# Chain of chunks: two engines' reads of one accumulator bank declared independent of each other

## The chip, the cores and the metric

The kernel runs on one core of a Trainium2 chip. The metric is the time of one execution in microseconds (us), as the device measures it. Before the change it is 1743.63 us (median of three runs, 1741.31 to 1744.07).

The engines are named as in the profile: PE is TensorE (its matmuls; PEld is its loading of weights), DVE is VectorE, ACT is ScalarE, POOL is GpSimd, SP is SyncE, which here only issues transfers. PE writes its products into accumulator banks; DVE and ACT read them out.

## The reference, cut to what matters

One layer of an encoder is computed for 1024 prompt frames and 64 sample frames: modulated norm, one input projection, two groups of heads (a delta-rule recurrence, "RWKV", and a forgetting attention, "FoX"), output projection, and a gated feed-forward network. The change lies in the recurrence, which for each of 8 heads is

```python
def step(s, inp):
    r_t, w_t, k_t, v_t, kk_t, a_t = inp
    sa = jnp.einsum('bhvk,bhk->bhv', s, -kk_t)
    s = (s * w_t[:, :, None, :]
         + sa[..., None] * (kk_t * a_t)[:, :, None, :]
         + v_t[..., None] * k_t[:, :, None, :])
    return s, jnp.einsum('bhvk,bhk->bhv', s, r_t)
...
ys_state = lax.scan(step, s0, xs)
...
x = x + gt1[:, None] * (jnp.concatenate([y_rwkv, y_fox], axis=-1) @ w_out)
ffn = (jax.nn.silu(h2 @ w_ffn_gate) * (h2 @ w_ffn_up)) @ w_ffn_down
```

`s` is a 64x64 state per head. The kernel computes the scan in chunks of 64 frames.

## The kernel before

**Halves and stages.** The frames are worked in two halves: half 0 has 512 (8 chunks), half 1 has 512 and the 64 sample frames (9 chunks, in matmuls of 288 columns). For each half the projections (L294 to L296, three products per tile because each factor is split in a high and a low part), the four pairs of RWKV heads, and the preparation of the attention are traced piece by piece, in an order that a string of letters gives. Then come attention, output projection (with attention of half 1), feed-forward and its last product (`pd`, L1264).

**The chain of chunks.** `rwkv_b` handles one pair of heads, `j`, of one half: the first head lies in partitions 0 to 63, the second in 64 to 127. After some preparation it walks over the chunks, and each chunk needs the state that the chunk before it left. There are 8 such chains (4 pairs, 2 halves), with 68 chunks in all. One chunk is, in the names of the program:

- `pR` (PE, L597), from the state and values `sv`; it is read out to `R`, the first head by DVE (L599), the second by ACT (L600);
- `pY` (PE, L608), a first part of the output, which nobody waits for at once;
- `pSA` (PE, L610), from `R`; it is read out into `sv`, the first head by DVE (L611), the second by ACT (L612);
- `pS` (PE, L613), from `sv`; DVE adds it twice (L617, one instruction a head) to the decayed state `sd`, which POOL has made (L604), and so writes the state for the next chunk;
- `pY` again (L618). After every fourth chunk `pY` is read out to `y`, one head by ACT and one by DVE (L623).

So each of `pR`, `pSA` and `pY` is one accumulator bank of which DVE reads one half of the partitions and ACT the other. 68 pairs of reads are at `pR`, 68 at `pSA`, 20 at `pY`.

**What sets the order.** The programming framework records the instructions, finds which must wait for which, and orders each engine's instructions with a list scheduler that works by its own estimate of when inputs are ready. Between the products of a chain it therefore puts other work on PE, above all projections (`pmm`) and, in the last chain, attention of half 0 (`psc`, `ppt`, `pav`). An engine then takes its instructions strictly in that order. Its rule for accumulator banks is that instructions of different engines on one bank are put in order, whatever partitions they touch: of the two reads of a pair, the second engine waits for the first.

Of the kernel before, what the change touches and what calls it, by code (L numbers as in the profile page):

```python
# [11 lines left out]
ALU = mybir.AluOpType  # L12
# [52 lines left out]
class K:  # L65
# [351 lines left out]
    def rwkv_a(self, hf, j, z, d):  # L417
# [79 lines left out]
                nc.sync.dma_start(d[0:ng].rearrange("g x s t -> (g x) s t")[:, o, o], t[r])  # L497
        return zv, rk, kb, pc, bon, At, dw, du

    def rwkv_b(self, hf, j, st):  # L500

        zv, rk, kb, pc, bon, At, dw, du = st
        nc, vc, O = self.nc, self.vc, self.O
# [57 lines left out]
        sv = self.rpool.tile([P, 9, 2, 64], F32, tag="sv", name="sv")  # L561
        S = self.state[j]
        for c in range(0, nch, 4):
            m = min(4, nch - c)
# [4 lines left out]
        for t0 in range(0, nch, 8):  # L569

            m = min(8, nch - t0)
# [9 lines left out]
        hsl = [slice(0, 64), slice(64, 128)]  # L581

        def put_state(c, src):
            nc.vector.tensor_copy(sv[hsl[0], c, 0], src[hsl[0]])
            nc.scalar.copy(sv[hsl[1], c, 1], src[hsl[1]])
        y = self.slot(name="y", tag="sb")
        put_state(0, S)
        py = None
        for c in range(nch):
            if c == 8:  # L590
                nc.sync.dma_start(O["state_p"][j], S)
                st = self.rpool.tile([P, 64], F32, tag="st", name="st")
                nc.sync.dma_start(st, self.A["state"][j])
                put_state(8, st)

            pr = self.ps([P, 2, 64], tag="ch", name="pR")
            nc.tensor.matmul(pr, At[:, c, 0], sv[:, c], start=True, stop=True)  # L597
            R = self.rpool.tile([P, 64], F32, tag="R", name="R")
            nc.vector.tensor_copy(R[hsl[0]], pr[hsl[0], 0])  # L599
            nc.scalar.copy(R[hsl[1]], pr[hsl[1], 1])  # L600

            sd = self.rpool.tile([P, 64], F32, tag="sd", name="sd")
            for h in range(2):
                nc.gpsimd.tensor_scalar(sd[hsl[h]], sv[hsl[h], c, h], pc[hsl[h], c], None, op0=ALU.mult)  # L604
            pS = self.ps([P, 2, 64], tag="ch", name="pS")
            if c % 4 == 0:
                py = self.ps([P, 4, 2, 64], tag="rb", name="pY")
            nc.tensor.matmul(py[:, c % 4], sv[:, c], rk[:, c], start=True, stop=False, skip_group_check=True)  # L608
            pa = self.ps([P, 64], tag="ch", name="pSA")
            nc.tensor.matmul(pa, inv[:, c], R, start=True, stop=True)  # L610
            nc.vector.tensor_scalar(sv[hsl[0], c, 0], pa[hsl[0]], -1.0, None, op0=ALU.mult)  # L611
            nc.scalar.mul(sv[hsl[1], c, 1], pa[hsl[1]], -1.0)  # L612
            nc.tensor.matmul(pS, kbt[:, c], sv[:, c], start=True, stop=True)  # L613
            last = c == 7 or c == nch - 1
            s0, s1 = (S[hsl[0]], S[hsl[1]]) if last else (sv[hsl[0], c + 1, 0], sv[hsl[1], c + 1, 1])
            for h, d in enumerate((s0, s1)):
                nc.vector.scalar_tensor_tensor(d, pS[hsl[h], h], pc[hsl[h], c], sd[hsl[h]], op0=ALU.mult, op1=ALU.add)  # L617
            nc.tensor.matmul(py[:, c % 4], sv[:, c], At[:, c, 1], start=False, stop=True, skip_group_check=True)  # L618
            if c % 4 == 3 or c == nch - 1:
                m = c % 4 + 1  # L620
                cb = c - m + 1
                for h, cp in enumerate((nc.scalar.copy, nc.vector.tensor_copy)):
                    cp(y[hsl[h], cb * 64:(c + 1) * 64].rearrange("p (c t) -> p c t", t=64), py[hsl[h], 0:m, h])  # L623
        if hf.smp:
            nc.sync.dma_start(O["state_s"][j], S)
        return y, bon
# [1075 lines left out]
```

## Time and profile before

| | |
|---|---|
| time, median of 3 runs | 1743.63 us (1741.31 to 1744.07) |
| the profiled execution's own time | 1735.94 us |
| its span, first to last instruction | 1734.2 us |
| PE, PEld busy | 1663.8 us (96%), 1447.9 us (83%) |
| DVE, ACT, POOL busy | 1126.6 us (65%), 729.1 us (42%), 180.8 us (10%) |
| mean granted PE clock | 0.981 |
| the 8 chains run from | 149 us to 728 us |

The profile is of one execution. In its listings a row of the timeline has start, duration, engine, line, operation, output<-inputs and shape, and in square brackets how long the engine had been idle and who ended that. In a list of waits a row reads: who waited, for whom, total us, how often, the longest. A waiting engine costs time only where work behind it is late for somebody. PE's busy time counts a matmul from its start to the end of its pipeline, so that consecutive matmuls overlap, and small gaps between starts are hidden in it.

### The profile page before, as it was taken

How to read it: one execution, taken by the hardware profiler on the slowest of the kernel's cores; microseconds unless marked ns; L12 is line 12 of the kernel's file. 1: busy time of each engine (PE TensorE's matmuls, PEld its weight loads, DVE VectorE, ACT ScalarE, POOL GpSimd, SP SyncE). 2: the span in 40 equal slices, each digit the busy share in tenths (PEclk: the TensorE clock that was granted, in tenths of full speed). 3: DMA queues.
4: the chain of work that ended last, by engine and by line, in shares of the span. 5: the costliest groups of instructions: out<-in, count | busy, mean ns of one | idle time of the engine just before them, and what ended most of it. 6: DMA issues, size and time to landing. Idle time of an engine off the chain costs nothing.

```text
span 1734.2 us, 33257 instructions
## 1 busy us (share of the span) xinstructions
PE 1663.8 (96%) x12893; PEld 1447.9 (83%) x12893; DVE 1126.6 (65%) x2574; ACT 729.1 (42%) x1532; POOL 180.8 (10%) x412
## 2 busy tenths in 40 slices
PE   5999999999999999889999989999999999999999
PEld 3676766688888888766888889999999999999998
DVE  6676676757686753876877686666666655555545
ACT  4534454553454445765776453333233223211210
POOL 2102121131221212300210000000000000000000
PEclk9999999999899999989999999999999999999999
DMA  8535457632233344566553333222222224433213
GB/s 314 149 95 137 142 140 207 175 93 56 55 76 75 95 121 136 157 194 177 151 177 136 127 115 101 75 75 75 76 75 82 78 87 143 161 98 98 95 37 122
DMA packets 133581, 207.09 MB, mean 119 GB/s; under 512 B 62126, under 2 KB 70350, under 8 KB 133422
## 3 DMA queue, kind: packets, MB, share of 16 engines
q1 hardware_dynamic: 133422, 204.95, 39.3%
q8 instruction: 102, 1.67, 0.4%
q14 instruction: 57, 0.47, 0.1%
HBM read 157.65 MB, written 47.25 MB: 118 GB/s over the span
## 4 chain that ended last, share of the span: by engine, by line
PE 82%; DVE 7%; ACT 7%; DMA 2%; issue 2%; SPq 1%; POOL 0%; DVEq 0%; ACTq 0%; POOLq 0%
PE pd L1264 15%; PE pfc L1153 8%; PE pfe L1153 8%; PE pfa L1153 7%; PE pmm L294 5%; PE pmm L296 5%; PE pmm L295 5%; PE pfb L1153 4%; PE pav L962 2%; PE pbs L375 2%; PE pA L464 2%; PE ppt L940 2%; PE po L294 1%; PE po L295 1%; PE po L296 1%
## 5 line engine op out<-in xcount | busy, mean ns | idle before, releaser
L294 PE MATMUL pmm<-hhi,whi 128*128 128x288 f32 (+1 forms) x624 | 220.7, 354 | 0.7 <-ACT pb L317 0.7
L295 PE MATMUL pmm<-hlo,whi 128*128 128x288 f32 (+1 forms) x624 | 218.2, 350 | 0.0
L296 PE MATMUL pmm<-hhi,wlo 128*128 128x288 f32 (+1 forms) x624 | 218.0, 349 | 0.0
L212 ACT CAST whi<-wraw 128x1024 fp32r<-128x1024 f32 (+2 forms) x116 | 99.3, 856 | 214.4 <-PE pd L1264 167.0
L1264 PE MATMUL pd<-ah,wlo 128*128 128x512 f32 (+1 forms) x528 | 173.5, 329 | 0.0
L1264 PE MATMUL pd<-al,whi 128*128 128x512 f32 (+1 forms) x528 | 173.2, 328 | 0.0
L1264 PE MATMUL pd<-ah,whi 128*128 128x512 f32 (+1 forms) x528 | 173.0, 328 | 0.0
L1268 DVE SCALAR_TENSOR_TENSOR x1t<-pd,mod,x1t 128x512 f32<-128x512 f32 x192 | 91.4, 498 | 110.6 <-PE pd L1264 110.0
L294 PEld LDWEIGHTS pmm<-hhi,whi 128*128 128x128 f32 x624 | 120.3, 193 | 13.5 <-ACT pb L317 2.0
L296 PEld LDWEIGHTS pmm<-hhi,wlo 128*128 128x128 f32 x624 | 120.3, 193 | 10.9 <-issue 1.7
L295 PEld LDWEIGHTS pmm<-hlo,whi 128*128 128x128 f32 x624 | 120.4, 193 | 9.6 <-issue 0.7
L216 DVE TENSOR_TENSOR wlo<-wraw,whi 128x1024 fp32r<-128x1024 f32 (+2 forms) x108 | 103.8, 961 | 26.0 <-ACT whi L212 25.6
L1153 PE MATMUL pfc<-hh,hS 128*128 128x256 f32 (+1 forms) x352 | 102.0, 290 | 4.4 <-ACT hh L1055 4.4
L1264 PEld LDWEIGHTS pd<-al,whi 128*128 128x128 f32 x528 | 99.4, 188 | 7.7
L1264 PEld LDWEIGHTS pd<-ah,whi 128*128 128x128 f32 x528 | 99.3, 188 | 7.7
L1264 PEld LDWEIGHTS pd<-ah,wlo 128*128 128x128 f32 x528 | 99.2, 188 | 7.4
L1153 PE MATMUL pfc<-hl,hS 128*128 128x256 f32 (+1 forms) x352 | 102.3, 290 | 0.0
L1153 PE MATMUL pfc<-hh,lS 128*128 128x256 f32 (+1 forms) x352 | 102.0, 290 | 0.0
L1153 PE MATMUL pfa<-hl,whi 128*128 128x256 f32 (+1 forms) x352 | 101.8, 289 | 0.0
L1153 PE MATMUL pfa<-hh,whi 128*128 128x256 f32 (+1 forms) x352 | 101.7, 289 | 0.0
L1153 PE MATMUL pfa<-hh,wlo 128*128 128x256 f32 (+1 forms) x352 | 101.4, 289 | 0.0
L604 POOL TENSOR_SCALAR sd<-sv,pc 64x64 f32<-64x64 f32 x136 | 72.0, 529 | 172.9 <-DVE sv L617 156.6
(360 smaller groups left out, 4402.0 us busy)
## 6 DMA issues: line engine op xcount, KB each, us to landing
wraw<-in_w_in_dram SPq DMA_DIRECT2D x52, 512.0 KB
wada<-in_w_ada_dram SPq DMA_DIRECT2D x48, 512.0 KB
as<-actscr SPq DMA_DIRECT2D x22, 544.0 KB
wraw<-in_w_gate_dram SPq DMA_DIRECT2D x22, 512.0 KB
wraw<-in_w_up_dram SPq DMA_DIRECT2D x22, 512.0 KB
wraw<-in_w_down_dram SPq DMA_DIRECT2D x40, 256.0 KB
wraw<-in_w_out_dram SPq DMA_DIRECT2D x16, 512.0 KB
actscr<-sg SPq DMA_DIRECT2D x22, 288.0 KB
```

The costliest lines, as they stand in the source:

```text
L212: nc.scalar.copy(hi, src)
L216: eng.tensor_tensor(lo, src, hi.bitcast(F32), op=ALU.subtract)
L294: nc.tensor.matmul(ps[0:M, 0:n], whi[:, k, 0:M], xhi[:, k, off:off + n], start=(k == 0), stop=False)
L295: nc.tensor.matmul(ps[0:M, 0:n], whi[:, k, 0:M], xlo[:, k, off:off + n], start=False, stop=False)
L296: nc.tensor.matmul(ps[0:M, 0:n], wlo[:, k, 0:M], xhi[:, k, off:off + n], start=False, stop=(k == kt - 1))
L375: nc.tensor.matmul(ps[:, 0:n], w, x[:, off:off + n], start=True, stop=True)
L464: nc.tensor.matmul(pa[h][:, i], kb[hp, c + i], rk[hp, c + i], start=True, stop=True)
L604: nc.gpsimd.tensor_scalar(sd[hsl[h]], sv[hsl[h], c, h], pc[hsl[h], c], None, op0=ALU.mult)
L940: nc.tensor.transpose(pt[0:rows, b - b0, t * P:t * P + qn], p[0:qn, pc:pc + rows], self.ident[0:qn, 0:qn])
L1153: nc.tensor.matmul(ps, l[:, k], r[:, s, k], start=(first and k == 0 and y == 0), stop=(k == 3 and y == 2), skip_group_check=True)
L1264: nc.tensor.matmul(ps[:, 0:n], w[:, i], x[:, t:t + n], start=(i == 0 and y == 0), stop=(i == len(fs) - 1 and y == 2))
L1268: nc.vector.scalar_tensor_tensor(dst, ps[:, so - off:so - off + l], self.mod[:, 40 + o, b:b + 1], dst, op0=ALU.mult, op1=ALU.add)
```

## The change

A helper declares to the framework that, of two instructions, neither has to wait for the other. It is applied to the three pairs of reads in the loop over the chunks. The instructions themselves, their shapes and their engines stay. Since the helper is new, lines behind it are 4 higher at first and 3 at the end: L597 becomes L601, both reads of `pR` (L599, L600) stand on L603, `pSA` is L613 and its reads L614 and L615, `pS` is L616, the state's update L620, `pY` is read at L625, and the attention's L910 is L913.

```diff
+    def apart(self, a, b):
+
+        self.tc.declare_no_dep(b.ins, a.ins, reason="different partition quarters of a bank")
+
...
             R = self.rpool.tile([P, 64], F32, tag="R", name="R")
-            nc.vector.tensor_copy(R[hsl[0]], pr[hsl[0], 0])
-            nc.scalar.copy(R[hsl[1]], pr[hsl[1], 1])
+            self.apart(nc.vector.tensor_copy(R[hsl[0]], pr[hsl[0], 0]), nc.scalar.copy(R[hsl[1]], pr[hsl[1], 1]))
...
             nc.tensor.matmul(pa, inv[:, c], R, start=True, stop=True)
-            nc.vector.tensor_scalar(sv[hsl[0], c, 0], pa[hsl[0]], -1.0, None, op0=ALU.mult)
-            nc.scalar.mul(sv[hsl[1], c, 1], pa[hsl[1]], -1.0)
+            self.apart(nc.vector.tensor_scalar(sv[hsl[0], c, 0], pa[hsl[0]], -1.0, None, op0=ALU.mult),
+                       nc.scalar.mul(sv[hsl[1], c, 1], pa[hsl[1]], -1.0))
...
-                for h, cp in enumerate((nc.scalar.copy, nc.vector.tensor_copy)):
-                    cp(y[hsl[h], cb * 64:(c + 1) * 64].rearrange("p (c t) -> p c t", t=64), py[hsl[h], 0:m, h])
+                self.apart(*[cp(y[hsl[h], cb * 64:(c + 1) * 64].rearrange("p (c t) -> p c t", t=64), py[hsl[h], 0:m, h])
+                             for h, cp in enumerate((nc.scalar.copy, nc.vector.tensor_copy))])
```

Because the scheduler places work by when it thinks inputs are ready, the change also moves instructions. All moves lie between the first chain and the end of the attention of half 0; ahead of the first chain (149 us) and behind about 780 us the engines' instructions stand as before, but for a few rows of attention in half 1.

On PE, in the sixth chain (pair 1 of half 1), the fifth chunk. What a row waits for stands in brackets: `Activation` is ACT, `Pool` is POOL, and each named engine is one semaphore to wait on. Before:

```order
L597 MATMUL pR<-sv,At 128x128 [waits DVE_49,PE_49]
L294 MATMUL pmm<-hhi,whi 128x288
L295 MATMUL pmm<-hlo,whi 128x288
L608 MATMUL pY<-rk,sv 128x128 [waits DVE_49]
L296 MATMUL pmm<-hhi,wlo 128x288
L610 MATMUL pSA<-R,inv_693 128x64 [waits Activation_49]
L294 MATMUL pmm<-hhi,whi 128x288
L295 MATMUL pmm<-hlo,whi 128x288
L296 MATMUL pmm<-hhi,wlo 128x288
L294 MATMUL pmm<-hhi,whi 128x288
L295 MATMUL pmm<-hlo,whi 128x288
L613 MATMUL pS<-sv,kb 128x128 [waits Activation_49]
```

The same chunk after the change:

```order
L601 MATMUL pR<-sv,At 128x128 [waits DVE_49,PE_49]
L296 MATMUL pmm<-hhi,wlo 128x288
L611 MATMUL pY<-rk,sv 128x128 [waits DVE_49,Activation_49]
L294 MATMUL pmm<-hhi,whi 128x288
L613 MATMUL pSA<-R,inv_693 128x64 [waits DVE_49,Activation_49]
L295 MATMUL pmm<-hlo,whi 128x288
L296 MATMUL pmm<-hhi,wlo 128x288
L294 MATMUL pmm<-hhi,whi 128x288
L616 MATMUL pS<-sv,kb 128x128 [waits DVE_49,Activation_49]
```

One projection of three is gone from between `pR` and `pSA`, and two of five from between `pSA` and `pS`; and `pSA` and `pS` now name both reading engines, where they named the later one. Over all 68 chunks, projections between `pR` and `pSA` go from 224 (67 of 512 columns, 157 of 288) to 170 (38 and 132), those between `pSA` and `pS` from 295 (91 and 204) to 227 (60 and 167), and other rows of PE there from 223 to 109.

On ACT, around the same chunk (`whi` is the high part of a weight tile, `pb` receives a projection). Before:

```order
L600 COPY R<-pR 64x64 [waits DVE_49,Activation_49]
L612 ACTIVATE sv<-pSA 64x64 [waits DVE_49,Pool_49]
L212 CAST whi<-wraw 128x1024 [waits DMAHW2_49,PE_49]
L317 COPY pb<-pmm 128x224 [waits PE_49]
L317 COPY pb<-pmm 128x64
```

And after:

```order
L603 COPY R<-pR 64x64 [waits PE_49,Activation_49]
L615 ACTIVATE sv<-pSA 64x64 [waits PE_49,Pool_49]
L212 CAST whi<-wraw 128x1024 [waits DMAHW1_49,PE_49]
L317 COPY pb<-pmm 128x224 [waits PE_49]
L317 COPY pb<-pmm 128x64
```

ACT's two reads now wait for PE's product and no longer for DVE. All 68 reads of `pR` and all 68 of `pSA` have changed so.

The third place is PE at the last projection of all, where the last chain (pair 3 of half 1) goes over from projections to attention beside it. Before:

```order
L295 MATMUL pmm<-hlo,whi 128x288
L296 MATMUL pmm<-hhi,wlo 128x288
L814 MATMUL pkv<-ident,fv 128x128 x2
L910 MATMUL psc<-k1x_8027,qsx_8025 128x256
L912 MATMUL psc<-k2x_8028,q2x_8026 128x256
L916 LDWEIGHTS identb
L916 MATMUL psc<-cmask,identb 128x128
L613 MATMUL pS<-sv,kb 128x128
```

And after:

```order
L295 MATMUL pmm<-hlo,whi 128x288
L296 MATMUL pmm<-hhi,wlo 128x288
L817 MATMUL pkv<-ident,fv 128x128
L601 MATMUL pR<-sv,At 128x128
L611 MATMUL pY<-rk,sv 128x128
L817 MATMUL pkv<-ident,fv 128x128
L913 MATMUL psc<-k1x_8027,qsx_8025 128x256
L915 MATMUL psc<-k2x_8028,q2x_8026 128x256
```

The `pS` before is that of the chain's first chunk; the `pR` after is that of its fourth. So three chunks stand ahead of the last projection where less than one stood, and six stand beside the attention where eight stood.

## The prediction, as put on record before the result

> **What bounds the kernel now.** I read the page's table of busy times and its chain of waits first, then the busy times by stretch.
>
> ```profile
> span 1734.2 us, 33257 instructions
> PE 1663.8 (96%) x12893; PEld 1447.9 (83%) x12893; DVE 1126.6 (65%) x2574; ACT 729.1 (42%) x1532; POOL 180.8 (10%) x412
> PE 82%; DVE 7%; ACT 7%; DMA 2%; issue 2%; SPq 1%; POOL 0%; DVEq 0%; ACTq 0%; POOLq 0%
> ...
> core 0: us, PE busy (x) PEld busy (x) DVE busy (x) ACT busy (x) POOL busy (x), PEclk, DMA share, GB/s
> 149.00:690.00 541.00, 524.79 (x4722) 422.85 (x4720) 358.81 (x975) 258.10 (x596) 116.39 (x236) 0.98 0.42 115
> 690.00:730.00 40.00, 35.47 (x237) 28.59 (x236) 33.11 (x116) 27.78 (x88) 13.30 (x34) 1.00 0.52 147
> 730.00:780.00 50.00, 42.30 (x218) 30.34 (x217) 38.63 (x104) 35.13 (x95) 3.74 (x21) 0.90 0.67 192
> 780.00:1734.20 954.20, 933.76 (x6627) 876.89 (x6625) 592.99 (x1117) 338.43 (x621) 25.41 (x40) 0.99 0.34 107
> ```
>
> PE holds 82% of the chain that ended last. The change touches the second stretch (seven chains beside projections, PE 97% busy, 16 us without a matmul), the third (the last chain beside attention, DVE 83% busy) and, by the order, the fourth. The last row, 954 us, stays as it is. PE's products are the same in number, so only waits of PE, shown or hidden between starts, can be won or lost. Next, who waits in the chain:
>
> ```profile
> ACT R L600 <- DVE R L599: 55.1, 38, 2.7
> ACT sv L612 <- DVE sv L611: 26.5, 31, 1.8
> PEld pS L613 <- ACT sv L612: 16.2, 47, 1.0
> PEld pSA L610 <- ACT R L600: 12.0, 41, 0.8
> PEld pR L597 <- issue: 8.6, 31, 0.5
> ...
> PE pS L613 <- ACT sv L612: 3.1, 7, 0.8
> ```
>
> ACT sat 81.6 us behind DVE's reads. That is ACT's time, and ACT is 42% busy. What PE lost to the second read is 28.2 us of idle weight loads in 88 places (16.2 + 12.0); the last row shows that only 3.1 us of the 16.2 appear as an idle PE, the rest hides under the product before. One chunk that nothing disturbs, in time (the fifth of the sixth chain, whose order of rows is shown above):
>
> ```profile
> 572.41 0.30 PEld L597 LDWEIGHTS pR<-sv,At 128*128 128x128 f32 x2 [0.23 <-PE pmm L296]
> 572.44 0.46 PE L597 MATMUL pR<-sv,At 128*128 128x128 f32 x2
> 572.65 0.38 PE L294 MATMUL pmm<-hhi,whi 128*128 128x288 f32 x1
> 572.94 0.22 DVE L599 COPY R<-pR 64x64 f32<-64x64 f32 x1 [0.20 <-PE pR L597]
> 573.14 0.38 PE L296 MATMUL pmm<-hhi,wlo 128*128 128x288 f32 x1
> 573.24 0.21 ACT L600 COPY R<-pR 64x64 f32<-64x64 f32 x1 [0.66 <-DVE R L599]
> 573.50 0.30 PEld L610 LDWEIGHTS pSA<-R,inv 128*128 128x128 f32 x2 [0.19 <-ACT R L600]
> 573.50 0.43 PE L610 MATMUL pSA<-R,inv 128*128 128x64 f32 x2
> 574.05 0.22 DVE L611 TENSOR_SCALAR sv<-pSA 64x64 f32<-64x64 f32 x1 [0.89 <-PE pSA L610]
> 574.23 0.29 PE L294 MATMUL pmm<-hhi,whi 128*128 128x288 f32 x1
> 574.36 0.22 ACT L612 ACTIVATE sv<-pSA 64x64 f32<-64x64 f32 x1 [0.91 <-DVE sv L611]
> 574.36 0.29 PE L295 MATMUL pmm<-hlo,whi 128*128 128x288 f32 x1
> 574.63 0.30 PEld L613 LDWEIGHTS pS<-sv,kb 128*128 128x128 f32 x2 [0.21 <-ACT sv L612]
> 575.90 0.46 PE L597 MATMUL pR<-sv,At 128*128 128x128 f32 x2
> ```
>
> The reader should see three things: DVE and ACT read one after the other, PE is fed by projections that start 0.13 us apart (574.23, 574.36), and it still stands idle a little at `pSA` (573.14 + 0.13 = 573.27, started at 573.50) and at `pS` (574.36 + 0.13 = 574.49, started at 574.63).
>
> **What the change takes from the chain.** From `pR`'s end (572.44 + 0.46 = 572.90) to `pSA`'s load, 0.60 us pass: 0.04 to DVE's start, 0.22, 0.08, 0.21 on ACT, 0.05. Side by side, ACT starts 0.04 to 0.10 us after `pR` (by a second semaphore, which its row in the order shows) and ends after 0.25 to 0.31; with the load's 0.05 that is 0.30 to 0.36, so 0.24 to 0.30 less. From `pSA`'s end (573.93) to `pS`'s load it is 0.70 us: 0.12, 0.22, 0.09, 0.22, 0.05. Side by side 0.12 + 0.22 + 0.05 = 0.39, so 0.31 less.
>
> **What it adds.** `pSA` and `pS` now wait for two engines. The nearest row is `pR`, which has two waits already:
>
> ```profile
> L597 PEldq EVENT_SEMAPHORE  x63: 51/51/51, 147.5 to 720.9; - x63
> ```
>
> 63 of its 68 have a separate wait of 51 ns in PE's queue. By the order 134 of the 136 `pSA` and `pS` get the same. Where the engine that this wait names ends first, it is hidden under the other's copy; where it ends last, the load comes about 0.06 us later. Bounds 0 and 134 x 0.06 = 8.0 us; I take half, 0.03 us a place, since the two copies are nearly equally long. That leaves savings of 0.24 and 0.28 us, 0.26 a place.
>
> **What moves.** The scheduler answers by taking work out from under the chain. Of 512-column projections 60 leave the two gaps ((67 - 38) + (91 - 60)), of 288-column ones 62, of other rows 114. The short ones cost 0.13 us each, as above; the long ones:
>
> ```profile
> 150.55 0.40 PE L295 MATMUL pmm<-hlo,whi 128*128 128x512 f32 x1
> 150.78 0.40 PE L296 MATMUL pmm<-hhi,wlo 128*128 128x512 f32 x1
> ```
>
> 0.23 us. For the others I take 0.11: `pR` starts at 572.44 and the projection behind it at 572.65, so one of `pR`'s two passes costs half of 0.21. Many of the rows are cheaper 32x32 products, some dearer attention products, so 0.05 to 0.2. The sum is 60 x 0.23 + 62 x 0.13 + 114 x 0.11 = 13.8 + 8.1 + 12.5 = 34 us (28 to 45), or 0.25 us at each of the 136 places. So chain and cover shrink alike: an undisturbed `pSA` or `pS` will wait about as long as now, 136 x (0.25 - 0.26) = -1.4 us, which I count as **0** (bounds -5 and +5). The 34 us of products run between the chains instead, at full rate, and are no gain by themselves.
>
> **What is left to win** is in disturbed places, where DVE or ACT comes late because other work stands ahead of it. Now both delays add; then only the greater counts. The chunk above idles 0.19 and 0.21 us at its two loads; 88 x 0.20 = 17.6 of the 28.2 us are of that kind, 10.6 us are above it. I take half of that, **-5** (bounds 0 and -10.6).
>
> **The stretch beside the attention** (690 to 780 us): three chunks move out of it. Each has two DVE reads and two updates, 0.22 + 0.22 + 0.60 us in the row below, so 3.1 us of DVE's 33.1, and five pairs of PE passes.
>
> ```profile
> 575.15 0.60 DVE L617 SCALAR_TENSOR_TENSOR sv<-pS,pc,sd 64x64 f32<-64x64 f32 x2 [0.89 <-PE pS L613]
> ```
>
> A pair of passes is the 0.21 us from above, so 5 x 0.21 x 3 = 3 us go to the projections' stretch, where PE is full, and DVE's 3.1 us at 83% busy, 3.7 us, leave this one if DVE sets its length, nothing if it doesn't. The two nearly cancel; I take **0** (bounds -3.7 and +3).
>
> The 20 pairs at `pY` are not on the path: their readers wait little.
>
> ```profile
> L623 DVE COPY y<-pY x20: 224/427/428, 165.9 to 728.0; 64x256 f32<-64x256 f32 x16, 64x64 f32<-64x64 f32 x4
> ...
>   PEld pbs L375: 0.9, 2
>   PEld pY L608: 0.8, 1
> ```
>
> Cover is the norm of the pair, traced much later; without it 0.43 us a pair would count at most, 8.6 us. I take 0.
>
> ACT's 81.6 us of freed waiting are worth nothing by themselves, since ACT then waits for `pR` or `pSA` in the same place in its queue. Nothing on ACT is queued behind a longer wait than before; on PE, the projections behind `pSA` and `pS` stand behind the second semaphore, which is priced above.
>
> **Sum**: 0 - 5 + 0 + 0 = -5 us, from the profiled execution's 1735.9 us to 1731. The profiled execution lies 7.7 us below the median of the runs shown (1743.63), so the same share there gives 1738.6; I say **1739**.
>
> **The rivals.** *No change* (within 0.2%, 3.5 us, about what a measurement of this kernel can tell from none): the scheduler gives the whole of it back, disturbed places included, because it has also cut the cover that caught a late DVE or ACT. For it: cover and latency fall by the same 0.25 us. Against it: two delays in a row are longer than one. 1743.
>
> *Slower by the double wait*: every `pSA` and `pS` pays the second semaphore behind its last reader, 134 x 0.06 = 8.0 us, and the disturbed places gain nothing. For it: `pR`, with two waits, idles 8.6 us "until issue" though DVE's update has ended. Against it: the separate wait is free when it names the earlier reader. It decides from about 60 of the 134 places on (3.5 / 0.06). 1743.6 + 8 = 1752.
>
> *Slower by collision*: two engines reading one bank at the same time slow each other, so that each copy takes 0.43 us, not 0.22. The chain is then as long as now, but its cover is gone: up to 34 us, 1778. In the rows above no two reads of a pair overlap, so they don't exclude it. [...] No run shown so far bears on it.
>
> *Larger gain*: disturbed places vanish altogether (-10.6) and the attention stretch gives its 3.7: -14, 1729. For it: the longest waits of ACT behind DVE are 2.7 and 1.8 us.
>
> **How the numbers follow.** Chances: forecast 0.34, larger gain 0.12, no change 0.27, double wait 0.22, collision 0.05. Faster by over 0.2%: 0.46; within: 0.27; slower: 0.27. The forecast's own range is 1730 to 1743 (-13 to 0). The range of all reaches from the larger gain to the double wait, and a little beyond, since moved rows are not priced one by one: 1726 to 1754. Left out: collision and the ends.
>
> **What would show it.** In the changed profile: no wait of ACT's reads for DVE, and the two reads of a pair overlapping, each still 0.21 to 0.22 us long (if 0.3 or more, collision). PEldq should have 134 more waits of 51 ns at L613 and L616. A chunk's period, 3.46 us in the rows above (572.44 to 575.90), should fall by about 0.5 where undisturbed. Idle of the loads at `pSA` and `pS`, 28.2 us now, should end at 18 to 26 us: above 30, the double wait or the lost cover rules; near 10, the larger gain. The stretch behind 780 us should last 954 us as now. I am wrong in kind if the time moves with that idle unchanged: then the moved projections decide, not the chain.

## The result, and the profile after

The changed kernel took 1756.20 us (median of 4 runs, 1749.58 to 1756.88) against 1742.87 us (1741.31 to 1744.07) in the same comparison: 1.0074 times the time, 95% interval 1.0051 to 1.0098. I had forecast 1739 us, and had given a slowdown of over 0.2% a chance of 0.27, as much as no change and less than a gain (0.46). The profiled execution of the change took 1749.58 us, its span is 1747.8 us, 13.6 us longer than that of before.

First the steps of the change itself. The rows of the groups by line, and one chunk in time with the starts of its neighbours, in the changed kernel:

```profile
L615 ACT ACTIVATE sv<-pSA 64x64 f32<-64x64 f32 x68 | 14.9, 220 | 35.8 <-PE pSA L613 31.3 <-POOL ns L329 2.5 <-POOL sd L607 1.0
L603 DVE COPY R<-pR 64x64 f32<-64x64 f32 x68 | 14.7, 216 | 49.4 <-PE pR L601 47.3 <-ACT whi L212 0.9
L614 DVE TENSOR_SCALAR sv<-pSA 64x64 f32<-64x64 f32 x68 | 14.6, 215 | 25.9 <-PE pSA L613 25.1 <-POOL ns L329 0.3
L603 ACT COPY R<-pR 64x64 f32<-64x64 f32 x68 | 14.1, 208 | 51.2 <-PE pR L601 50.4
```

```profile
560.99 0.46 PE L601 MATMUL pR<-sv,At 128*128 128x128 f32 x2
...
564.11 0.46 PE L601 MATMUL pR<-sv,At 128*128 128x128 f32 x2
564.66 0.21 ACT L603 COPY R<-pR 64x64 f32<-64x64 f32 x1 [1.88 <-PE pR L601]
564.68 0.22 DVE L603 COPY R<-pR 64x64 f32<-64x64 f32 x1 [0.71 <-PE pR L601]
565.01 0.30 PEld L613 LDWEIGHTS pSA<-R,inv 128*128 128x128 f32 x2 [0.18 <-ACT R L603]
565.04 0.41 PE L613 MATMUL pSA<-R,inv 128*128 128x64 f32 x2
565.54 0.22 ACT L615 ACTIVATE sv<-pSA 64x64 f32<-64x64 f32 x1 [0.67 <-PE pSA L613]
565.56 0.21 DVE L614 TENSOR_SCALAR sv<-pSA 64x64 f32<-64x64 f32 x1 [0.66 <-PE pSA L613]
565.89 0.30 PEld L616 LDWEIGHTS pS<-sv,kb 128*128 128x128 f32 x2 [0.22 <-ACT sv L615]
567.16 0.46 PE L601 MATMUL pR<-sv,At 128*128 128x128 f32 x2
```

ACT no longer waits for DVE but for PE (50.4 and 31.3 us of its idle time end with `pR` and `pSA`). The two reads lie over each other (564.66 and 564.68; 565.54 and 565.56) and are no longer for it: 0.208 and 0.216 us in the mean. A chunk takes 3.12 and 3.05 us here (560.99, 564.11, 567.16), against 3.46 in the chunk that the prediction showed; part of that is cover that left, since 11 and 10 projections run in these two and 12 in that one. The idle time of the loads that wait for the reads, by the table of waits of the same kernel:

```profile
PEld pS L616 <- ACT sv L615: 11.9, 40, 0.9
...
PEld pSA L613 <- ACT R L603: 7.9, 29, 1.3
```

That is 19.8 us, where it was 28.2. So far all is in kind as forecast, and the time got longer. The busy times by stretch tell where. The stretches end where the projections end, and where the output projection begins (after the change 0.7 us between the first two are left out); first before, then the change:

```profile
149.00:692.20 543.20, 526.99 (x4736) 424.76 (x4735) 359.90 (x978) 259.05 (x599) 116.39 (x236) 0.98 0.41 114
692.20:778.70 86.50, 74.27 (x431) 56.06 (x429) 69.35 (x213) 60.68 (x177) 17.05 (x55) 0.94 0.62 178
778.70:1734.20 955.50, 935.06 (x6634) 877.84 (x6632) 594.29 (x1119) 339.70 (x623) 25.41 (x40) 0.99 0.34 107
```

```profile
149.00:705.70 556.70, 546.65 (x4757) 446.14 (x4757) 360.24 (x988) 260.53 (x603) 122.27 (x241) 0.93 0.40 111
706.40:790.60 84.20, 69.23 (x401) 50.56 (x398) 66.58 (x201) 57.83 (x172) 13.89 (x50) 0.98 0.61 182
790.60:1747.80 957.20, 937.06 (x6634) 879.25 (x6632) 594.56 (x1119) 339.74 (x624) 25.36 (x40) 0.99 0.34 107
```

The stretch of chains beside projections is 13.5 us longer; the other two differ by -2.3 and +1.7. In it PE is busy 19.7 us more (546.65 against 526.99) with nearly the same number of matmuls (4757 against 4736), and idle less (10.1 us against 16.2). The column before the last two says why the same products take longer: the granted TensorE clock fell from 0.98 to 0.93. The changed kernel does wait less. Its PE runs at half clock for longer.

In the clock records of the two profiled executions the granted share is 1 or 0.5, and no value between. The half-clock stretches last 3.41 us (6 of them), 6.83 (13), 10.24 (3), 17.07 and 20.48, so 1 to 6 times 3.41 us, but for the last of each record, which its end cuts off. The products agree with these records. In such a stretch of the changed kernel 288-column projections start 0.24 us apart, and 0.13 us at full clock:

```profile
619.00 0.44 PE L296 MATMUL pmm<-hhi,wlo 128*128 128x288 f32 x1
619.24 0.44 PE L294 MATMUL pmm<-hhi,whi 128*128 128x288 f32 x1
```

The longest stretch of the changed kernel, in steps of 3.41 us:

```profile
458.30:461.70 3.40, 3.40 (x53) 2.94 (x52) 3.37 (x7) 1.47 (x3) 0.90 (x3) 1.00 0.23 37
461.70:465.10 3.40, 2.97 (x37) 2.11 (x38) 3.37 (x7) 0.53 (x2) 0.43 (x2) 1.00 0.02 5
465.10:468.50 3.40, 3.40 (x146) 3.20 (x143) 2.79 (x8) 2.19 (x6) 0.10 (x1) 1.00 0.56 159
468.50:471.90 3.40, 3.40 (x58) 2.90 (x57) 2.01 (x2) 0.78 (x2) 3.13 (x4) 0.51 0.40 116
471.90:475.40 3.50, 3.50 (x21) 2.66 (x19) 0.35 (x1) 1.37 (x3) 1.05 (x2) 0.50 0.31 122
...
485.60:489.00 3.40, 3.40 (x16) 3.40 (x17) 1.94 (x6) 0.22 (x1) 0.69 (x2) 0.50 0.18 19
489.00:492.40 3.40, 3.37 (x25) 2.96 (x25) 1.88 (x7) 1.99 (x5) 0.70 (x3) 1.00 0.08 22
```

From 465.1 to 468.5 PE is busy for the whole time, with 146 products, and then the clock halves, for 20.5 us. What PE does in that window are 32x32 products (`pg`, `pw`, `pu`, `pgt` in `small`, which prepare a chain): `32*32` of the array in their rows, where a projection has `128*128`: one sixteenth. After them come `f32` products `pA` and transposes of other pairs, and few projections.

### The profile page after: what moved, and what is told of

It reads as the page before. It is cut to its first block, busy times and chain, and to the rows that moved or that the text cites. A ratio compares the mean times of both kernels' runs of the same rounds, so it can differ in the third digit from the quotient of the medians.

```text
span 1747.8 us, 33421 instructions
## 1 busy us (share of the span) xinstructions
PE 1682.3 (96%) x12893; PEld 1466.3 (84%) x12893; DVE 1125.0 (64%) x2574; ACT 728.6 (42%) x1532; POOL 184.1 (11%) x412
## 4 chain that ended last, share of the span: by engine, by line
PE 84%; ACT 5%; DVE 5%; DMA 3%; issue 1%; SPq 0%; DVEq 0%; ACTq 0%; POOL 0%
PE pd L1267 15%; PE pfe L1156 7%; PE pfc L1156 7%; PE pfa L1156 7%; PE pmm L294 5%; PE pmm L296 5%; PE pmm L295 5%; PE pfb L1156 4%; PE pbs L375 3%; PE pav L965 2%; PE pA L464 2%; PE ppt L943 2%; PE po L294 1%; PE po L295 1%; PE po L296 1%
## 5 line engine op out<-in xcount | busy, mean ns | idle before, releaser
L294 PE MATMUL pmm<-hhi,whi 128*128 128x288 f32 (+1 forms) x624 | 224.9, 361 | 1.6 <-ACT hhi L271 0.9
L295 PE MATMUL pmm<-hlo,whi 128*128 128x288 f32 (+1 forms) x624 | 223.0, 357 | 1.2 <-DVE hlo L272 1.2
L296 PE MATMUL pmm<-hhi,wlo 128*128 128x288 f32 (+1 forms) x624 | 223.5, 359 | 0.0
L294 PEld LDWEIGHTS pmm<-hhi,whi 128*128 128x128 f32 x624 | 124.4, 199 | 15.5 <-ACT pb L317 2.8
L295 PEld LDWEIGHTS pmm<-hlo,whi 128*128 128x128 f32 x624 | 124.4, 199 | 11.9 <-DVE hlo L272 1.6
L296 PEld LDWEIGHTS pmm<-hhi,wlo 128*128 128x128 f32 x624 | 124.1, 199 | 10.6 <-issue 1.9
```

Source lines behind the costliest of these rows:

```text
L294: nc.tensor.matmul(ps[0:M, 0:n], whi[:, k, 0:M], xhi[:, k, off:off + n], start=(k == 0), stop=False)
L295: nc.tensor.matmul(ps[0:M, 0:n], whi[:, k, 0:M], xlo[:, k, off:off + n], start=False, stop=False)
L296: nc.tensor.matmul(ps[0:M, 0:n], wlo[:, k, 0:M], xhi[:, k, off:off + n], start=False, stop=(k == kt - 1))
```

## Theories

**Clock theory**: the waits that went away are a gain, as forecast; the order that the scheduler chose in answer lets PE's clock fall to half for longer, and that costs more. **Wait theory**: the waits themselves cost (the second semaphore, the reads side by side). **Stall theory**: the new order costs by stalls, and the clock is only a companion.

## Experiment 1: the order without the change, the change without the order

Each kernel is built twice. The first pass gives the order of the instructions on each engine; the second is held to it by edges that carry no wait. `own` says whether the three declarations are made. All comparisons in this and the next sections are with the kernel before on the same chip (1742.24, 1743.36 and 1742.24 us).

```diff
     def apart(self, a, b):
-        self.tc.declare_no_dep(b.ins, a.ins, reason="different partition quarters of a bank")
+        if self.own:
+            self.tc.declare_no_dep(b.ins, a.ins, reason="different partition quarters of a bank")
...
+    def follow(tc, instructions, order):
+        by = {x.name: x for x in instructions}
+        edge = mybir.DependencyInfo(mybir.DependencyClass.NoSync, mybir.DependencyReason.DATA)
+        for names in order.values():
+            names = [n for n in names if n in by]
+            for a, b in zip(names, names[1:]):
+                tc.add_manual_dep(by[b], a, edge, reason="the other kernel's order")
...
+    nc = traced(True, order_of(traced(False, None)))
```

The last line is that of `order_before`; `order_after` has `traced(False, order_of(traced(True, None)))`.

> The three declarations with the instruction order of the kernel before on every engine; nothing else changes. Clock theory (the removed waits are a gain, and the changed order costs because PE runs longer on nothing but 32x32 products ahead of the chains, and its granted clock falls): clock back at about 0.98, faster than before, 1715 to 1738 us. Wait theory (the double waits and the side-by-side reads cost): 1750 us or more at a clock of 0.98. Stall theory (the changed order costs by stalls of engines, the clock is only a companion): faster than before too, 1715 to 1738; this run separates it from the wait theory only.

> The instruction order of the changed kernel on every engine, with the waits between the reads as before; no declaration. Clock theory: clock 0.96 to 0.97 as in the changed kernel, and the chain's longer waits with less cover, so slower than the changed kernel: 1760 to 1790 us. Wait theory: at most 1748, since the double waits are gone. Stall theory: 1760 to 1790.

`order_before`: 1735.57 us, 0.9971 of before (0.9953 to 0.9990). `order_after`: 1781.40 us, 1.0219 (1.0200 to 1.0238). Both lie where the clock theory put them, and the wait theory has fallen. The stall theory gave the same ranges and is not touched by these two runs. The gains: with the order held, the removed waits gain 6.7 us in one order and 25 us in the other (1781.4 to 1756.2). The moved order costs 20.6 us with the declarations (1735.6 to 1756.2; 18 us by the two ratios to before) and 39 without. The loads' idle time, first in `order_before`, then in `order_after` (the lines are shifted by 1 to 5):

```profile
PEld pS L617 <- ACT sv L616: 10.3, 26, 1.0
...
PEld pSA L614 <- ACT R L604: 5.4, 17, 0.6
```

```profile
PEld pS L617 <- ACT sv L616: 25.5, 54, 1.2
PEld pSA L614 <- ACT R L604: 20.4, 57, 0.7
```

The span and mean clock of the four kernels, each from its view by cores (before, `order_before`, after, `order_after`):

```profile
core 0: 1734.2 us, clock 0.981
```

```profile
core 0: 1729.1 us, clock 0.978
```

```profile
core 0: 1747.8 us, clock 0.968
```

```profile
core 0: 1775.7 us, clock 0.967
```

A stretch at half clock loses at most half its length to one at full clock, and that only where the products are the bound (0.24 us against 0.13 above is a little less than half). So (1 - clock) x span is an upper bound of the loss. Against before:

| kernel | loss by the clock at most, us | idle at `pSA` and `pS`, us | sum of the two against before | span against before |
|---|---|---|---|---|
| before | 32.9 | 28.2 | | |
| `order_before` | 38.0 | 15.7 | 5.1 - 12.5 = -7.4 | -5.1 |
| after | 55.9 | 19.8 | 23.0 - 8.4 = +14.6 | +13.6 |
| `order_after` | 58.6 | 45.9 | 25.7 + 17.7 = +43.4 | +41.5 |

Two numbers account for all four spans within 2.3 us. That is bookkeeping, not yet a cause: the clock could still be a companion of something else, and the first column is an upper bound (experiment 5 shows by how much it can be too high).

A second price of the clock comes from one and the same kernel. Its runs differ in clock: of 19 runs of before in the last comparison the one at 0.972 took 1747.8 us and one at 0.980 took 1737.9 us, 1.24 us per 0.001; a line through all 19 gives 1.43 (correlation -0.96), one through the 12 of `order_before` 1.35 (-0.96). The other two comparisons' runs of before give 1.27 and 1.75. At 1.3 us, the 0.012 between the median clocks of `order_before` (0.9755) and after (0.9635) are 15.6 of the 20.6 us (15 to 21 with 1.27 to 1.75); the 4.1 us more of idle loads could be most of the rest.

## Experiment 2: full products strewn among the small ones

If the clock falls for want of large products, adding some should hold it up. One bf16 product, of 128 rows and columns of the array and 224 columns of data, was put behind each chunk's 32x32 products (272 in all), and as a control the same on 32 rows and columns.

```diff
-                        nc.tensor.matmul(pg[h][r, c], *mm(h, c, r, slice(32 * x, 32 * x + 32)), start=True, stop=True)
+                        self.last = nc.tensor.matmul(pg[h][r, c], *mm(h, c, r, slice(32 * x, 32 * x + 32)), start=True, stop=True)
+                if self.warm and c % 1 == 0:
+                    one = self.ident.bitcast(BF16)
+                    d = nc.tensor.matmul(pg[1][0:128, 9:16].rearrange("p c t -> p (c t)"), one[0:128, 0:128],
+                                         one[0:128, 0:224], start=True, stop=True)
+                    self.extra.append((self.last.ins, d.ins))
```

> The changed kernel, in its order, with 272 added bf16 products of the full 128x128 array by 224 columns, one after each chunk's 32x32 products ahead of the chains; they write columns of a bank that nothing reads, and are no part of the reference. By the 0.13 us of a 288-column projection they cost 0.10 to 0.15 us each, 27 to 41 us in all. Clock theory: the stretches at half clock ahead of the chains (about 70 us of them in the changed kernel between 149 and 700 us) shrink to under 20 us, the granted clock reaches 0.98, and 20 to 25 us of the cost come back: 1758 to 1777 us. Stall theory: the half clock or the stalls stay, 1783 to 1797. Wait theory: 1783 to 1797.

> As the run with 272 added products of the full array, but each uses 32 rows and 32 columns of the array, with the same 224 columns moved, so the same time in the queue with a sixteenth of the array at work. Clock theory, if what counts is how much of the array works: clock at most 0.965 as in the changed kernel, 1783 to 1797 us. If what counts is that PE moves columns at all, the clock rises here as in the run with the full array, and both take the same time. Stall and wait theories: 1783 to 1797, the same as the run with the full array.

Measured: 1873.61 us for the full ones (clock of the profiled run 0.940), 1765.00 us for the small ones (0.968). Both are misses. In the first the clock fell further, and the cost was 117 us instead of 27 to 41. The second lies 18 us below the 1783 to 1797 that the three theories gave it: its products cost 9 us. By its timeline, at full clock:

```profile
139.54 0.27 PE L531 MATMUL pg<-ident 128*128 128x224 bf16 x1
139.74 0.25 PE L528 MATMUL pg<-gt,At 32*32 32x32 f32 x4
139.92 0.27 PE L531 MATMUL pg<-ident 128*128 128x224 bf16 x1
140.12 0.25 PE L528 MATMUL pg<-gt,At 32*32 32x32 f32 x4
140.30 0.27 PE L531 MATMUL pg<-ident 128*128 128x224 bf16 x1
```

A product of 288 full columns starts 0.13 us after its like, yet from the full product of 224 columns to the first small one 0.20 us pass, and from there, over four small passes, 0.18 us to the next full one. Over all records of before, a 32x32 product comes 224 ns after a 288-column one (133 ns when another large one follows), and a large one 121 ns after a small one (25 ns when another small one follows): about 0.19 us for going to small products and back. The control stays in 32x32 and has no such change-over; that this is why it was cheaper is an inference. By these prices the 272 full products bought some 52 us of change-overs (272 x 0.19), and the clock did not hold. The test had mixed two things, and was made again in blocks (experiment 5).

**What counts as use.** The 14 profiled kernels of this study can be asked directly. For each 3.41 us window I added up, over the records of its matmuls, columns x share of rows x share of columns of the 128x128 array, and divided by the window's length: full columns per us, the use. For scale: the 512-column row of the prediction, 0.23 us, is a use of 2226 at full clock, and 288 columns in 0.24 us are 1200 at half clock. No view groups this; it is counted from the records, and the counts hang by a few windows on how a product across a border is shared out:

| window at full clock, use in full columns per us | windows | followed by half clock |
|---|---|---|
| below 360 | 78 | 70 |
| 360 to 600 | 131 | 71 |
| 600 to 840 | 283 | 49 |
| 840 and more | 6105 | 0 |

| window at half clock, use in full columns per us | windows | followed by half clock |
|---|---|---|
| below 540 | 167 | 156 |
| 540 to 840 | 138 | 89 |
| 840 and more | 131 | 1 |

So a stretch of half clock began in these executions after a window of little use of the array (190 of the 492 below 840, none of the 6105 from there on). It seldom ended after a window below 540 (11 of 167), and nearly always after one of 840 or more (130 of 131). Little use is not always an idle PE: in 26 of the 78 windows below 360 PE was busy for over 97% of the time, and 18 of these 26 were followed by half clock; in the others it stood idle in part. The strewn products fit in: in the 13 full-clock windows of that kernel with six or more of them the use is some 600 in the median, and 8 of the 13 were followed by half clock.

Between 149 and 700 us before and after have nearly the same number of full-clock windows below 600 (7 and 8), but 2 of the 7 and 6 of the 8 were followed by half clock. Before has 3 stretches of half clock there, 7 windows in all, the longest of 3; after has 8 stretches, 22 windows, the longest of 6. `order_before` has 4 stretches of 7 windows, `order_after` 8 of 18. So in the changed order PE falls more often and stays down longer. Each count is of one execution, and the windows lie differently against the program in each: their grid begins 2.01 us behind the first instruction in before, 0.91 us in after. Which of the moved products makes the difference is not shown by these counts.

## Experiment 3: projections moved towards the small products, and away

I took from the counts that what stands right behind the small products decides. Two kernels bring projections forward to that place, one puts them off.

```diff
+        names, large = order[str(mybir.EngineType.PE)], set(large)
+        for end, ahead in zip(ends, AHEAD):
+            at = names.index(end) + 1
+            for n in [n for n in names[at:] if n in large][:ahead]:
+                names.remove(n)
+                names.insert(at, n)
+                at += 1
```

`end` is the last 32x32 product of a chain. `late_before` takes the products between `end` and the first `pR` instead and puts them behind that `pR`.

> The changed kernel, in its order, but in six of the eight chains up to 32 projection products (10, 32, 32, 32, 28, 14) that follow the last of the 32x32 products stand right behind it, ahead of the transposes and the f32 products pA; nothing is added. Clock theory as it stands after the first runs (PE's half clock begins after a stretch of little array use and ends only after a stretch of much; the changed order left little large work behind the 32x32 products): half clock between 149 and 700 us falls from 75 us to under 48, granted clock 0.970 or more, and, with up to 5 us lost because the first chunks of the chains have less cover, 1740 to 1752 us. Stall theory: less cover and nothing for it, 1756 to 1766 us at any clock.

> The three declarations in the order of the kernel before (1735.6 us), but some of the projection products (5, 3, all, all, 10, 20, 20, 10 at most) that stand between the last 32x32 product and the first pR of a chain come right behind that pR; nothing is added, no chain loses cover. Clock theory: half clock between 149 and 700 us grows from 24 us to 40 or more, granted clock 0.971 or less, 1741 to 1752 us. Stall theory: 1733 to 1738 us, as without the move.

> The three declarations in the order of the kernel before, and up to 32 projection products (14, 32, 32, 28, 32, 32 in six chains) put forward right behind the last 32x32 product. Clock theory: there is only 24 us of half clock to shorten between 149 and 700 us, so clock 0.976 to 0.981 and, against up to 5 us of lost cover, 1729 to 1738 us. Stall theory: the lost cover alone, 1736 to 1745 us.

`late_before`: 1749.63 us, 1.0043 of before (1.0024 to 1.0062), clock 0.971, 13 half-clock windows between 149 and 700 us (44 us) where `order_before` has 7. That is what the clock theory gave, and not what the stall theory gave. How much of it is the clock, the two prices answer differently: 6 of the 14.1 us between the medians (0.0045 x 1300), or 12.7 of the 18.8 us between the profiled spans ((1 - 0.971) x 1747.9 - 38.0). Idle at `pR` grew by 3.8 us besides (12.4 against 8.6), so stalls have a part in it.

`early_after`: 1759.29 us (1.0092, 1.0069 to 1.0115). `early_before`: 1755.83 us (1.0074, 1.0048 to 1.0100). Both are misses of the clock theory. The first lies in the range of the stall theory (1756 to 1766), the second beyond that of either. The clock hardly rose in the first (median 0.9695 against 0.9635; 18 half-clock windows instead of 22) and fell in the second (0.9715 against 0.9755; 17 instead of 7). The profile of `early_after` shows what the move broke:

```profile
PEld pkbt L574 <- ACT kb L575: 4.8, 7, 1.0
...
PEld pkbt L574 <- ACT inv L558: 2.3, 4, 0.6
PEld pvt L582 <- ACT kb L575: 2.3, 4, 0.9
```

These rows are from 149 to 716 us. The projections had lain between the transposes `pkbt` and `pvt` and covered ACT's copies there. Taken from there they leave 9.4 us of idle loads where the changed kernel has 2.7 (1.1, 0.6 and 1.0 in the same rows), and the clock halves again: between 149 and 700 us the stretches of half clock became shorter (10 with 18 windows, against 8 with 22), but more. That the gaps behind the moved products are the reason was not tested. So moving projections costs by stalls too, and that large products right behind the small ones hold the clock is not shown.

## Experiment 4: one declaration alone

```diff
-            nc.vector.tensor_copy(R[hsl[0]], pr[hsl[0], 0])
-            nc.scalar.copy(R[hsl[1]], pr[hsl[1], 1])
+            self.apart(nc.vector.tensor_copy(R[hsl[0]], pr[hsl[0], 0]), nc.scalar.copy(R[hsl[1]], pr[hsl[1], 1]))
```

This edit of the kernel before, with the helper, declares `pR` alone; the other two likewise. The scheduler orders each anew.

> Of the three declarations only that on the readers of pR, in the order that the scheduler then chooses. The removed wait is worth about half of the 6.7 us that all three are worth in the order of before. Clock theory: 1739 - 1300 x (clock - 0.976), within 6 us. Stall and wait theories: the time has no relation to the clock.

> Of the three declarations only that on the readers of pSA, in the order that the scheduler then chooses. The removed wait is worth about half of the 6.7 us that all three are worth in the order of before. Clock theory: 1739 - 1300 x (clock - 0.976), within 6 us. Stall and wait theories: the time has no relation to the clock.

> Of the three declarations only that on the readers of pY, whose waits lie off the path; the order of the instructions is again the scheduler's own, and it differs from both kernels' (some 1,750 of PE's instructions stand elsewhere than before). Clock theory: the time follows the clock of the new order at 1.3 us per 0.001, so 1742 - 1300 x (clock - 0.976), within 5 us, whatever the clock comes out as. Wait theory: within 3.5 us of the kernel before at any clock.

| declared | time, us | ratio to before | median clock | expected at that clock |
|---|---|---|---|---|
| `pR` | 1734.03 | 0.9959 (0.9935 to 0.9984) | 0.9745 | 1735 to 1747 |
| `pSA` | 1747.41 | 1.0017 (0.9992 to 1.0043) | 0.968 | 1743 to 1755 |
| `pY` | 1748.86 | 1.0040 (1.0018 to 1.0062) | 0.975 | 1738 to 1748 |
| all | 1756.20 | 1.0074 (1.0051 to 1.0098) | 0.9635 | |

Two of three lie just outside what the clock alone gave (by 1 us or less, on opposite sides), so the clock does not explain the last 6 us. Between kernels it explains less than that sounds: `pR` and `pY` have nearly the same median clock and lie 14.8 us apart, of which the idle loads at `pSA` and `pS` (19.4 and 24.6 us) can be 5; the rest stays open. For the profiled executions of the three, the bookkeeping of experiment 1 gives -7, +21 and +16 us against before, and the spans differ by -7, +17 and +18. Within each kernel the time follows the clock of the run at 1.23 to 1.42 us per 0.001 (correlations -0.96, -0.97 and -0.99). A declaration that removes waits off the path, `pY`, makes the kernel slower, by 5.5 us at a median clock 0.001 lower. The wait theory (within 3.5 us) has fallen here too. What is left to explain it is that the scheduler chose another order; what in that order costs is not shown.

## Experiment 5: blocks of full products, and of small ones

To change the clock and nothing else: 480 added products in blocks of 12, one block behind each of the five groups of 32x32 products of a chain, so that change-overs are few. Order, waits, places and columns are the same in both kernels; only the rows and columns of the array at work differ, 128 or 32.

```diff
+        def block(last, pg):
+
+            one = self.ident.bitcast(BF16)
+            for _ in range(12 if self.warm else 0):
+                d = nc.tensor.matmul(pg[1][0:128, 9:16].rearrange("p c t -> p (c t)"), one[0:128, 0:128],
+                                     one[0:128, 0:224], start=True, stop=True)
+                self.extra.append((last.ins, d.ins))
+                last = d
```

> The changed kernel, in its order, with 480 added bf16 products of the full 128x128 array by 224 columns, in blocks of 12: one block behind each of the five groups of 32x32 products of a chain, so that every window of 3.4 us there has at least a block of full use. They write columns that nothing reads and are no part of the reference. By the 288-column row they cost some 0.1 us each, 48 us in all, and 40 changes between 32x32 and full products 8 us more. Clock theory, in which what counts is how much of the array works in a window: half clock between 149 and 700 us falls from 75 us to under 25, granted clock 0.975 or more, 1770 to 1790 us, and 20 to 40 us less than with the same blocks on a sixteenth of the array. Stall theory: both blocks cost alike, 1800 to 1815 us, and the clock doesn't rise.

> The same 480 added products in the same blocks and places, with the same 224 columns each, but on 32 rows and 32 columns of the array, a sixteenth of it. Clock theory: clock at most 0.965, half clock between 149 and 700 us as long as in the changed kernel or longer (75 us and more), 1800 to 1815 us. If moving columns is what counts, or stalls alone, the time is that of the full blocks or some 8 us less.

Full blocks: 1771.69 us (1.0162, 1.0137 to 1.0187). Small blocks: 1815.96 us (1.0418, 1.0381 to 1.0454). The first falls in the range of the clock theory, the second 1 us beyond it, and their difference is 4 us above the 20 to 40 expected. From 149 us to the end of the projections, first with full blocks, then with small ones:

```profile
149.00:724.80 575.80, 565.35 (x5202) 463.93 (x5200) 364.29 (x1007) 266.06 (x616) 120.28 (x241) 0.99 0.40 110
```

```profile
149.00:763.30 614.30, 604.81 (x5197) 491.50 (x5197) 364.45 (x1002) 265.90 (x615) 120.03 (x241) 0.90 0.37 103
```

With nearly the same number of products, PE is busy 39.5 us longer in the second, at a clock of 0.90 instead of 0.99. By count 2 windows at half clock are left between 149 and 700 us with full blocks, 29 with small ones. The kernel that puts sixteen times the array to work is 44 us faster, though at the same clock the added products cost alike: by count they start 0.096 us apart in both at full clock, and 0.187 us apart at half clock. That the clock is only a companion of stalls, which gave both the same time, has fallen: with order and waits held, the clock alone costs time. The price is 1.23 us per 0.001 (44.3 us over the median clocks 0.986 and 0.950), or 1.4 if the 8 us of change-overs that the small blocks spare are added, an estimate. The bookkeeping of experiment 1 gives 60 us for this pair (85.0 - 24.8) where the spans differ by 38, so it can be well too high. Moving columns alone did not hold the clock here: both kernels move the same columns, at 0.99 and 0.90, and in the window from 489.5 us of the small blocks the use is by count some 140 full columns per us, and the next is at half clock.

The change itself, held in this way from falling, is not a faster kernel, since the blocks cost more than they save: 1756.2 + 48 (the estimate of 0.1 us each) - 1771.7 = 32 us saved. Both kernels are beaten by two others: `order_before` (1735.57 us) and the declaration at `pR` alone (1734.03 us).

## Why the prediction was wrong

- **Latency.** Right in kind. In the chunk above, from `pR`'s end (564.57) to `pSA`'s load 0.44 us pass, 0.16 less than before (0.24 forecast); from `pSA`'s end (565.45) to `pS`'s load 0.44, 0.26 less (0.28 forecast).
- **Double wait.** Mis-sized. The 134 waits are there, 67 in each row:

```profile
L613 PEldq EVENT_SEMAPHORE  x67: 51/51/51, 149.0 to 724.8; - x67
L616 PEldq EVENT_SEMAPHORE  x67: 51/51/51, 150.1 to 725.6; - x67
```

  The load starts 0.11 and 0.12 us after the later read ends (564.90 to 565.01, 565.77 to 565.89), against 0.05 before, so where the two reads end together the second wait costs 0.06 to 0.07 us. Counted over the loads that stood idle, the median is 0.115 us at both places, where it was 0.051. I had taken 0.03, half of my bound.
- **Undisturbed and disturbed places.** The sum was -5; the idle time at `pSA` and `pS` fell by 8.4 us, to 19.8, inside the 18 to 26 that I had named. So these terms were of the right size for the waits. That `order_before` gains 6.7 us, near the 5 forecast, confirms nothing: the sum counted the undisturbed places as 0 because their cover shrinks, and in that order it doesn't. By the same working their 17.6 us should have gone there too, with half of the 10.6; 12.5 of the 28.2 us went, and the time fell by half of that.
- **The step that failed**: "The 34 us of products run between the chains instead, at full rate, and are no gain by themselves." That they leave was right: without the declarations the same order has 45.9 us of idle loads, 17.7 more. "At full rate" was not: over the stretch of the chains the mean clock was 0.93, not 0.98, with 22 windows at half clock between 149 and 700 us where there had been 7. Which of the moved work had kept the clock up is not shown. The sum had no term for the clock, though the rows that I quoted have it in their PEclk column: 0.98 for 149 to 690 us, 0.90 for 730 to 780. That term is at most +23 us between the two profiled executions, against -8.4 of the waits; with the declarations held, the order costs 20.6 us, some 15 to 17 of them by the clock (0.012 at 1.23 to 1.43 us per 0.001).
- **Attention stretch, `pY`.** 86.5 us became 84.2, inside -3.7 to +3. The waits at `pY` are indeed off the path, but declaring it alone cost 0.4%, for which the order that followed is left as the reason.
- **Rivals.** Double wait (1752 us) came nearest in time and was not the cause: `order_before` has the same declarations and is faster. Collision is excluded, since reads side by side last 0.21 to 0.22 us as before. The last sentence, that I am wrong in kind if the time moves with that idle unchanged, because then the moved projections decide, pointed to the right place, though its condition was not met: the idle fell and the time rose.
- **The range** (1726 to 1754 us) missed by 2 us. Its bounds were those of waits and semaphores; none was the price of another order.

Open stays how much of the 20.6 us between the two orders is something else than the clock. Single runs give 15.6 for the clock, the blocks of experiment 5 about the same (0.012 at 1.23 to 1.4), the bookkeeping at most 17.9 (55.9 - 38.0) beside 4.1 of waits, and the kernels of experiments 3 and 4 show that another order can also cost by more than the clock. Also open is which part of the changed order lets the clock fall.

## What to carry to other kernels

Where an edit lets a scheduler reorder, price the new order apart from the edit: hold the order and make the edit, then hold the edit and make the order. Read the granted clock by stretch before and after; here PE's busy time grew by 19.7 us while its products stayed nearly the same in number (4757 against 4736), and that pointed to the clock (0.93 against 0.98), not to waiting. Beside small-tile products, blocks of large ones held the clock here (0.986 over the span); strewn ones did not (0.940), and cost more than they gave, and moving projections forward did not pay.

## What the runs showed of the hardware that I had not expected

- PE, busy without a gap (3.40 of 3.40 us from 465.1 us of the changed kernel), fell to half clock when its products used little of the array. Below 360 full columns per us in a 3.41 us window the next was at half clock in 70 of 78 cases (18 of the 26 in which PE was busy for over 97% of the window), from 840 on in none of 6105. It came back in 130 of 131 cases after a window of 840 or more at half clock, and in 11 of 167 below 540.
- Going from full products to 32x32 ones and back cost about 0.19 us in before (224 - 133 + 121 - 25 ns), more than a 288-column product (0.13 us).
- The spread of single runs of this kernel went with the clock (correlation -0.96 over 19 runs): 0.972 to 0.980 and 1747.8 to 1737.9 us. The records put the windows on a grid that stood otherwise against the program in the two profiled runs of before and after: it begins 2.01 and 0.91 us behind the first instruction.
- A second wait on a PE instruction cost 0.06 to 0.07 us where both events came together (0.115 against 0.051 us from the later read to the load).
